# A residue subtraction moved from VectorE to GpSimd for weight pieces of the second block

## The chip, the cores and the metric

The kernel runs on one core of one Trainium2 chip. The metric is the device time of one execution in microseconds (us); less is better. The engines named below are PE (TensorE matmul), PEld (its weight load), DVE (VectorE), ACT (ScalarE), POOL (GpSimd) and SP (SyncE, which only issues transfers here).

## The reference, cut to what matters

Two transformer-like blocks run one after the other on 256 positions of 1024 features, all in float32. The change lies in the mixer of the second block:

```
proj = h @ w_in                     # 1024 x 8224
glu_a, glu_b, q, k, v, z, a_in, b_in, gate_a, gate_b = split_cols(proj, IN_SIZES)
c = glu_a * sigmoid(glu_b)
c = depthwise_conv(c, conv_dw_w) + conv_dw_b          # 31 taps, 1024 channels
c = silu(layer_norm(c)); y_conv = c @ w_conv_out
qkv = silu(depthwise_conv(concat[q, k, v], qkv_conv_w))   # 5 taps
q, k, v -> l2_norm -> gated_delta_rule, forwards and backwards, 8 heads
o = rms_norm(o_fwd + o_bwd) * silu(z); y_delta = o @ w_delta_out
x = x + (sigmoid(gate_a) * y_conv + sigmoid(gate_b) * y_delta) @ w_o
```

## The kernel before, in words

**Weights.** Every weight matrix comes in pieces of 128 x 2048 floats (1 MB): 256 output columns, with the 1024 input features as 8 groups of 128. `Weights.raw` (L177) issues the transfer of a piece on SP (L187) into a `raw` buffer. `Weights.new` (L200) splits the piece into two parts that are multiplied apart: ACT casts `raw` to `hi` (L211), and `lo = raw - hi` is formed on DVE (L212). With `parts=2`, as in the second block, each of these is done in two instructions of 128 x 1024. PE then multiplies both (`mmA`, tiles `mmA<-xs,hi` and `mmA<-xs,lo`): 48 matmuls per piece. In the second block there are two buffers each for `raw`, `hi` and `lo`. A raw buffer can take its next piece once the last reader of the piece before it, which is the second `lo` instruction, has ended. Pieces listed in `NATIVE` are multiplied straight from `raw`.

**Order.** `SEQ` (L33) lists the steps of the second block. A letter is a kind of step and a digit a pair of heads or channels: `g` gates a pair of conv channels (pieces b and a, `glu`), `k` the keys, `p` the queries and values (pieces q and v), `i` the inverse for two heads, `d` the delta rule for two heads, `v` the 31-tap convolution of one tile of 128 channels (`conv31`, taps at L1341), `z`, `x`, `y` gates, `u` the norm of the output, `o` its projection, `l` the norm of the convolution. The entries `rv0`, `rb2`, `rb3`, `rz2` fetch and split a piece ahead of its use: the loop calls `W.split("in2", 2)` itself there and keeps the result in the dictionary `ahead`, from which the inner `split(key)` (L1048) takes it later. The part of the list that matters is `... p1 i0 rb2 g2 i1 d0 v0 p2 v1 i2 d1 rb3 g3 p3 i3 d2 ...`.

The order of instructions on an engine is not that of the code. When the program is built, a planner takes instructions by their place in the code and by costs and due times of its own, so that, for example, the taps of the convolution (L1341) stand between instructions of other steps. Once built, each engine works through its list in order.

**What else is near.** In `inverse(i)` POOL has one `affine_select` for each head (L1185), which sets a diagonal in `U`; ACT copies of it (L1188) and the first matmul of the inverse wait for it. These eight selects are all that POOL does between 631 us and the end of the block. The steps of the inverse go from PE to ACT and DVE and back (`Z` at L1200, `X` at L1208). The `qkv` convolution has its taps at L1078. `ln_y` (L1129 to L1133) is a logarithm over 128 x 32 values. At the end of the block `conv_norm` takes the mean of the convolution with the matmuls `mu<-cv,onesm`, which need all taps.

Of the kernel before, what the change touches and what calls it, by code (L numbers as in the profile page):

```python
# [10 lines left out]
F32 = mybir.dt.float32  # L11
# [4 lines left out]
OP = mybir.AluOpType  # L16
# [17 lines left out]
z0 u0 u1 u2 v2 u3 v5 y0 y1 v3 y2 y3 o v7 l x0 x1 x2 x3""".split()  # L34

NATIVE = ("b0", "a0", "q0", "q1", "z1", "q2", "z0", "k0")
XF, XE, XO, XL = 1, 1, 1, 1
XR = 1
P_NAT, P_UP, P_DN, P_OUT, P_ODD = 2, 1, 2, 2, 2
# [12 lines left out]
def weight_spec():  # L52

    w8 = lambda n, cols: [(n, 0, 8, c, 256) for c in cols]
    halves = lambda n, k0: [(n, k0, 4, 0, 512), (n, k0, 4, 512, 512)]
    s = [("even_in", 0, 8, 1792, 68)] + w8("even_in", (1536, 1860, 2116, 2372, 2628, 2884, 3140))
    s += w8("even_in", (0, 256, 512, 768, 1024, 1280))
    s += halves("even_out", 4) + halves("even_out", 0)
    s += up_down("up0", "down0")
    s += w8("odd_in", (1544,)) + [("odd_in", 0, 8, 1536, 8)] + w8("odd_in", (1800, 2056)) + w8("odd_in", range(0, 1536, 256))  # L60
    s += halves("odd_out", 4) + halves("odd_out", 0)
    s += up_down("up1", "down1")
    first = {"g": "ba", "k": "k", "p": "qv", "z": "z", "x": "x", "y": "y"}
    col = {"a": 0, "b": 1024, "q": 2048, "k": 3072, "v": 4096, "z": 5120, "x": 6176, "y": 7200}
    piece = lambda key: w8("in2", [col[key[0]] + 256 * int(key[1])])
    for q in SEQ:
        if q[0] == "r":
            s += piece(q[1:])
        for c in first.get(q[0], ""):
            if "r" + c + q[1] not in SEQ:  # L70
                s += piece(c + q[1])
        if q == "e":
            s += [("in2", 0, 8, 6144, 32)]
        if q == "o":
            s += w8("delta_out", range(0, 1024, 256))
    s += w8("conv_out", range(0, 1024, 256))
    s += w8("o", range(0, 1024, 256))
    u = up_down("up2", "down2")
    s += u[:2] + [("pl_proj", 0, 2, 0, 1024)] + u[2:]
    s += w8("pl_gate", range(0, 1024, 256))  # L80
    return s
# [72 lines left out]
class Weights:  # L154
# [39 lines left out]

        self.ready.append(self.new(name, parts))

    def split(self, name, parts=1, moving=False):
        return self.ready.pop(0) if self.ready else self.new(name, parts, moving)

    def new(self, name, parts, moving=False):  # L200
        r = self.raw(name)
        nk, w = r.shape[1], r.shape[2]
        hp, lp, kw = self.rings()
        hi = hp.tile([128, WBUF], FR, tag="hi", name=f"hi{self.i}", **kw)
        lo = lp.tile([128, WBUF], FR, tag="lo", name=f"lo{self.i}", **kw)
        o = SWAP if moving else 0
        hi, lo = (t[:, o:o + nk * w].rearrange("p (k c) -> p k c", k=nk) for t in (hi, lo))
        n = -(-nk // parts)
        for a in range(0, nk, n):
            b = min(nk, a + n)  # L210
            self.nc.scalar.copy(hi[:, a:b], r[:, a:b])  # L211
            self.nc.vector.tensor_tensor(lo[:, a:b], r[:, a:b], hi[:, a:b].bitcast(F32), OP.subtract)  # L212
        return hi, lo


# [1 line left out]
def emit(ctx, tc, A):  # L217
    nc = tc.nc
# [9 lines left out]
    W = Weights(nc, A["wts"], weight_spec(), pool("raw", 2), pool("hi", 2), pool("lo", 2))  # L228
# [162 lines left out]
    def rstd_cols(*parts, eps=EPS):  # L391
        m, r = small(2, "rm"), small(2, "rs", 3)
        V.tensor_scalar(m, mean_cols(*parts), eps, None, OP.add)
        rsqrt(r, m, 2)
        return r
# [304 lines left out]
    with ExitStack() as st:  # L700
# [31 lines left out]
        r = rstd_cols(acc)  # L732
# [109 lines left out]
    with ExitStack() as st:  # L842
# [9 lines left out]
        r = rstd_cols(acc)  # L852
# [85 lines left out]
    with ExitStack() as st:  # L938
# [27 lines left out]
        scaled, ahead, turn = [], {}, []  # L966
# [79 lines left out]
            return e  # L1046

        def split(key):  # L1048
            return ahead.pop(key) if key in ahead else W.split("in2", 2)

        def proj(key):

            native = key in NATIVE
            w = W.raw("in2") if native else split(key)
            ps = bank("mm", "mmA")
            for m in range(2):
                if native:
                    mmN(ps[:, T * m:T * m + T], w, hg, m)
                else:
                    mmA(ps[:, T * m:T * m + T], w, xs1, m)  # L1060
            return ps
# [431 lines left out]
    with ExitStack() as st:  # L1493
# [40 lines left out]
        r = rstd_cols(acc)  # L1534
# [87 lines left out]
```

## Time and profile before

| | |
|---|---|
| median of 3 runs | 1235.45 us (1234.9 to 1237.3) |
| the profiled execution's own time | 1236.36 us |
| its span in the trace | 1234.6 us |
| mean granted TensorE clock | 0.991 of full speed |
| DMA over the span | 195.43 MB, mean 158 GB/s |

The span is the stretch from the first to the last instruction of the profiled execution; the execution's own time has 1.8 us around it. Times in the rows are us from the start of the span. A row of the timeline gives the start, the duration, the engine, the line, the operation, the tiles (out<-in), the shape and how many instructions are merged in it; in brackets stands idle time before it and what ended that.

### The profile page before, as it was taken

The numbers are of one execution on the slowest core, as the hardware profiler recorded it, in microseconds if no ns is written. First come the engines' busy times: TensorE is split into PE (matmuls) and PEld (weight loads), VectorE is DVE, ScalarE is ACT, GpSimd is POOL, SyncE is SP. The second block draws the span as 40 slices with busy tenths as digits, with TensorE's granted clock in tenths as the row PEclk, the third lists the DMA queues.
The fourth block names the chain that finished last, engine by engine and source line by source line (L and its number), as shares of the span: only waits on it lengthen the run. The fifth ranks groups of instructions, "written<-read, shape, count | busy, mean of one in ns | idle before, by whom it ended". The sixth has DMA issues, their size and how long they took to land.

```text
span 1234.6 us, 25022 instructions
## 1 busy us (share of the span) xinstructions
PE 1203.5 (97%) x10426; PEld 1149.7 (93%) x10426; DVE 967.8 (78%) x1926; ACT 714.4 (58%) x1185; POOL 12.5 (1%) x21
## 2 busy tenths in 40 slices
PE   8999999999999999999999999999999999999997
PEld 8978899999989899999989998989899999999996
DVE  5986798885597689787559898889998688666556
ACT  4565666664465566665426498898545565444444
POOL 0000000000000000000010000000000000000000
PEclk7999999999999999999999999999999999999999
DMA  5544355545343255555425323212244456555542
GB/s 223 210 150 163 111 205 205 191 173 201 129 169 137 103 205 175 200 187 189 170 81 196 113 105 136 70 36 71 102 137 171 171 201 218 190 204 191 189 167 86
DMA packets 29345, 195.43 MB, mean 158 GB/s; under 512 B 3504, under 2 KB 4016, under 8 KB 9136
## 3 DMA queue, kind: packets, MB, share of 16 engines
q1 hardware_dynamic: 29232, 193.83, 44.3%
q8 instruction: 82, 1.34, 0.4%
q14 instruction: 31, 0.25, 0.1%
HBM read 192.77 MB, written 1.05 MB: 157 GB/s over the span
## 4 chain that ended last, share of the span: by engine, by line
PE 67%; issue 11%; DVE 8%; ACT 5%; POOL 1%; DMA 0%; ACTq 0%; POOLq 0%; DVEq 0%
PE mmU L286 26%; PE mmD L286 15%; PE mmA L286 11%; PE mmB L286 3%; DVE lo L212 3%; PE mmO L286 3%; ACT hi L211 2%; PE mmF L286 2%; PE sr L286 1%; PE do L286 1%; PE at_y L286 1%; PE at_t L289 1%; ACT xbd L1217 1%; PE at_s L286 1%; DVE cv L495 0%
## 5 line engine op out<-in xcount | busy, mean ns | idle before, releaser
L211 ACT CAST hi<-raw 128x1024 fp32r<-128x1024 f32 (+2 forms) x281 | 337.0, 1222 | 299.0 <-PE mmU L286 119.5
L212 DVE TENSOR_TENSOR lo<-raw,hi 128x1024 fp32r<-128x1024 f32 (+2 forms) x281 | 400.5, 1438 | 113.3 <-ACT hi L211 112.6
L286 PE MATMUL mmU<-xs,hi 128*128 128x256 f32 x1996 | 356.2, 278 | 1.9 <-ACT hi L211 1.0
L286 PEld LDWEIGHTS mmU<-xs,hi 128*128 128x128 f32 x1996 | 306.4, 188 | 2.4 <-ACT hi L211 1.1
L286 PE MATMUL mmU<-xs,lo 128*128 128x256 f32 x1056 | 292.9, 278 | 1.4 <-DVE lo L212 1.4
L286 PE MATMUL mmA<-xs,hi 128*128 128x256 f32 x1152 | 220.0, 287 | 0.3 <-ACT hi L211 0.3
L286 PEld LDWEIGHTS mmU<-xs,lo 128*128 128x128 f32 x1056 | 198.2, 188 | 1.9 <-DVE lo L212 1.8
L286 PEld LDWEIGHTS mmA<-xs,hi 128*128 128x128 f32 x1152 | 179.1, 189 | 2.4 <-issue 0.7
L286 PE MATMUL mmD<-hid,hi 128*128 128x256 f32 x1008 | 177.2, 277 | 0.0
L286 PE MATMUL mmA<-xs,lo 128*128 128x256 f32 x576 | 163.1, 283 | 1.3 <-DVE lo L212 1.3
L286 PEld LDWEIGHTS mmD<-hid,hi 128*128 128x128 f32 x1008 | 153.6, 188 | 0.0
L286 PE MATMUL mmD<-hid,lo 128*128 128x256 f32 x528 | 146.1, 277 | 0.0
L286 PEld LDWEIGHTS mmA<-xs,lo 128*128 128x128 f32 x576 | 108.5, 188 | 3.4 <-DVE lo L212 1.9
L1341 DVE SCALAR_TENSOR_TENSOR cv<-cpad,par,cv 128x256 f32<-128x256 f32 x240 | 107.9, 480 | 0.5
L286 PEld LDWEIGHTS mmD<-hid,lo 128*128 128x128 f32 x528 | 99.1, 188 | 0.0
L286 PE MATMUL mmB<-hi,xs 128*128 128x256 f32 x416 | 75.9, 282 | 0.0
L286 PEld LDWEIGHTS mmB<-hi,xs 128*128 128x128 f32 x416 | 64.4, 190 | 0.7 <-issue 0.3
L286 PE MATMUL mmA<-hg,raw 128*128 128x256 f32 x256 | 63.9, 386 | 0.1
L495 DVE SCALAR_TENSOR_TENSOR cv<-mmU,par,cv 128x255 f32<-128x255 f32 (+1 forms) x144 | 61.4, 476 | 1.6 <-ACT cv L493 1.3
L286 PE MATMUL mmB<-lo,xs 128*128 128x256 f32 x208 | 58.6, 282 | 0.0
L286 PEld LDWEIGHTS mmA<-hg,raw 128*128 128x128 f32 x256 | 45.7, 190 | 5.3 <-issue 0.3
L286 PE MATMUL mmO<-xs,hi 128*128 128x256 f32 x256 | 48.0, 286 | 0.5 <-ACT xs L326 0.5
(452 smaller groups left out, 1783.5 us busy)
## 6 DMA issues: line engine op xcount, KB each, us to landing
raw<-in_wts_dram SPq DMA_DIRECT2D x157, 1024.0 KB, 4.8
raw<-in_wts_dram SPq DMA_DIRECT2D x24, 896.0 KB, 4.5
at_l<-in_relb_dram SPq DMA_DIRECT2D x4, 384.0 KB, 9.2
h<-in_xT_dram SPq DMA_DIRECT2D x4, 256.0 KB, 4.0
out_dram<-xg SPq DMA_DIRECT2D x2, 512.0 KB, 2.9
cst<-in_cst_dram SPq DMA_DIRECT2D x1, 640.0 KB, 8.5
buf<-in_g_plp_dram SPq DMA_DIRECT2D x1, 512.0 KB, 5.5
gfin<-in_g_fin_dram SPq DMA_DIRECT2D x1, 512.0 KB, 5.2
```

The source lines that it names most:

```text
L211: self.nc.scalar.copy(hi[:, a:b], r[:, a:b])
L212: self.nc.vector.tensor_tensor(lo[:, a:b], r[:, a:b], hi[:, a:b].bitcast(F32), OP.subtract)
L286: PE.matmul(out, lhsT=lhsT, rhs=rhs, start=start, stop=stop, skip_group_check=True)
L289: PE.transpose(out, in_, ident)
L495: V.scalar_tensor_tensor(y[:, d:], x[:, :T - d], cw[:, 3 * ch + 2 - d:3 * ch + 3 - d], y[:, d:], OP.mult, OP.add)
L1217: S.copy(XT[half[q], :, half[q]], py[half[q]].rearrange("p (n c) -> p n c", n=8))
L1341: V.scalar_tensor_tensor(cv[:, k], cpad[:, k, t:t + T], cw[:, t:t + 1], cv[:, k], OP.mult, OP.add)
```

## The change

A tuple `POOLED` names six pieces of the second block's input projection. `new` and `split` get an argument `eng`, the engine of the `lo` subtraction, which is DVE where it is not given. The inner `split(key)` passes GpSimd for keys in `POOLED`.

```
+POOLED = ("b2", "a2", "v2", "b3", "a3", "v3")
...
-    def split(self, name, parts=1, moving=False):
-        return self.ready.pop(0) if self.ready else self.new(name, parts, moving)
-
-    def new(self, name, parts, moving=False):
+    def split(self, name, parts=1, moving=False, eng=None):
+        return self.ready.pop(0) if self.ready else self.new(name, parts, moving, eng)
+
+    def new(self, name, parts, moving=False, eng=None):
...
-            self.nc.vector.tensor_tensor(lo[:, a:b], r[:, a:b], hi[:, a:b].bitcast(F32), OP.subtract)
+            (eng or self.nc.vector).tensor_tensor(lo[:, a:b], r[:, a:b], hi[:, a:b].bitcast(F32), OP.subtract)
...
         def split(key):
-            return ahead.pop(key) if key in ahead else W.split("in2", 2)
+            return ahead.pop(key) if key in ahead else W.split("in2", 2, False, nc.gpsimd if key in POOLED else None)
```

## Rows read from the trace of the kernel before

**Rows 1.** Windows of the second block: length, then busy us by engine.

```profile
710.00:800.00 90.00, 86.89 (x970) 78.56 (x968) 80.42 (x172) 79.75 (x162) 4.29 (x5) 1.00 0.30 106
800.00:910.00 110.00, 108.66 (x1120) 98.28 (x1119) 100.31 (x253) 78.75 (x150) 2.12 (x3) 1.00 0.20 72
938.00:965.00 27.00, 25.54 (x198) 24.33 (x197) 21.79 (x42) 18.24 (x29) 0.00 (x0) 1.00 0.38 125
```

**Rows 2.** DVE's timeline: lo instructions: b2 (second), a2, v2 (second), a3 (first), v3.

```profile
717.00 1.23 DVE L212 TENSOR_TENSOR lo<-raw,hi 128x1024 fp32r<-128x1024 f32 x1
...
718.99 2.36 DVE L212 TENSOR_TENSOR lo<-raw,hi 128x1024 fp32r<-128x1024 f32 x2
...
738.11 1.22 DVE L212 TENSOR_TENSOR lo<-raw,hi 128x1024 fp32r<-128x1024 f32 x1
...
761.72 1.22 DVE L212 TENSOR_TENSOR lo<-raw,hi 128x1024 fp32r<-128x1024 f32 x1
...
787.77 2.35 DVE L212 TENSOR_TENSOR lo<-raw,hi 128x1024 fp32r<-128x1024 f32 x2
```

**Rows 3.** POOL's timeline: three of the eight selects of the inverse.

```profile
727.96 0.64 POOL L1185 TENSOR_SCALAR_AFFINE_SELECT U<-U 128x512 f32<-128x512 f32 x1 [3.99 <-DVE U L1181]
...
761.87 1.56 POOL L1185 TENSOR_SCALAR_AFFINE_SELECT U<-U 128x512 f32<-128x512 f32 x1 [1.51 <-DVE U L1181]
...
838.04 0.75 POOL L1185 TENSOR_SCALAR_AFFINE_SELECT U<-U 128x512 f32<-128x512 f32 x1 [35.34 <-DVE U L1181]
```

**Rows 4.** DVE's timeline: one operation with and without a select beside it.

```profile
838.20 0.61 DVE L354 TENSOR_TENSOR nw_t<-nw_t,nw_m 128x4 f32<-128x4 f32 x1
...
845.46 0.15 DVE L354 TENSOR_TENSOR nw_t<-nw_t,nw_m 128x4 f32<-128x4 f32 x1
```

**Rows 5.** ACT's timeline: hi casts of a2, v2 (both), a3 (first), v3.

```profile
713.63 2.00 ACT L211 CAST hi<-raw 128x1024 fp32r<-128x1024 f32 x2 [0.18 <-DMA raw<-in_wts_dram]
...
726.84 1.05 ACT L211 CAST hi<-raw 128x1024 fp32r<-128x1024 f32 x1
...
736.78 1.05 ACT L211 CAST hi<-raw 128x1024 fp32r<-128x1024 f32 x1
...
752.84 1.05 ACT L211 CAST hi<-raw 128x1024 fp32r<-128x1024 f32 x1
...
786.40 2.00 ACT L211 CAST hi<-raw 128x1024 fp32r<-128x1024 f32 x2
```

**Rows 6.** DVE's timeline: what runs just after those casts.

```profile
715.03 0.19 DVE L1131 TENSOR_TENSOR ln_y<-ln_y,ln_b 128x32 f32<-128x32 f32 x1
...
727.80 1.01 DVE L1251 TENSOR_TENSOR E<-qk,E 128x384 f32<-128x384 f32 x2
728.73 0.48 DVE L1341 SCALAR_TENSOR_TENSOR cv<-cpad,par,cv 128x256 f32<-128x256 f32 x1
...
739.84 3.64 DVE L1341 SCALAR_TENSOR_TENSOR cv<-cpad,par,cv 128x256 f32<-128x256 f32 x9
...
753.66 1.22 DVE L212 TENSOR_TENSOR lo<-raw,hi 128x1024 fp32r<-128x1024 f32 x1
...
755.18 0.48 DVE L1341 SCALAR_TENSOR_TENSOR cv<-cpad,par,cv 128x256 f32<-128x256 f32 x1
...
790.05 3.25 DVE L1341 SCALAR_TENSOR_TENSOR cv<-cpad,par,cv 128x256 f32<-128x256 f32 x8
794.37 0.16 DVE L1303 COPY oss<-oss 128x4 f32<-128x4 f32 x1 [1.07 <-PE oss L286]
```

**Rows 7.** PE's timeline: b2's lo matmul, the mean's matmuls.

```profile
718.28 0.39 PE L286 MATMUL mmA<-xs,lo 128*128 128x256 f32 x1
...
937.58 3.61 PE L286 MATMUL mu<-cv,onesm 128*128 128x256 f32 x16
```

**Rows 8.** DVE's timeline: the last tap of the convolution.

```profile
937.61 0.48 DVE L1341 SCALAR_TENSOR_TENSOR cv<-cpad,par,cv 128x256 f32<-128x256 f32 x1
```

**Rows 9.** Waits of SP's queue, 710 to 800 us: total us, times, longest.

```profile
SPq L187 <- DVE lo L212: 98.0, 8, 25.6
```

## The prediction

> **What bounds the kernel now.** I read the windows first, then DVE's, POOL's and ACT's timelines around the weight pieces that the change names, then PE's at the places where it needs them, and last the waits of SP's queue. In the windows of the second block no engine stands out: from 710 to 800 us PE is busy 86.89 of 90 us, DVE 80.42 and ACT 79.75 [rows 1]. The inverse and the delta rule hand results from PE to ACT and DVE and back, projections fill PE between them, and convolution taps fill DVE. So PE is close to its limit and DVE is the engine behind it; the PE idle time that could be won back is 3.11 us there and 1.46 us from 938 to 965 us [rows 1]. At the end of the block the two run level: the mean of the convolution starts on PE at 937.58 us and the last tap on DVE at 937.61 us, ending at 938.09 [rows 7, 8]. POOL has 4.29 us of work in 90 [rows 1].
>
> **What really moves.** `POOLED` has six keys, but `b2` and `b3` are fetched by the entries `rb2` and `rb3`. There the loop calls `W.split("in2", 2)` without an engine, and the inner `split(key)` then only takes the finished piece from `ahead`. So these two stay on DVE, and a2, v2, a3 and v3 move: four pieces, eight instructions of 128 x 1024. No transfer is added, and no arithmetic. The transfer that waits for a `lo` to release its raw buffer now waits for POOL instead. SP already waits 98.0 us for `lo` in that stretch, eight times [rows 9]. Of the casts that I use below only one waited for its transfer, 0.18 us [rows 5]; the others wait for buffers and for ACT's own turn, so I charge nothing for a transfer that starts a little later. If that cover were gone, each of the four pieces could delay a cast by what POOL needs more than DVE, some 1.3 us.
>
> **What DVE saves.** The pair of a2 takes 2.36 us and so does that of v3 (2.35); a single one takes 1.22 [rows 2]. Next instructions start a little before the last ends, so I count 1.14 for each. Seven of them give 7.95 us. The eighth, v2's second at 738.11 [rows 2], stands before an idle moment of DVE, which waits for PE there, so its going saves nothing.
>
> **What POOL needs for one.** The trace has no two-input operation on POOL. The nearest row is the select, 0.64 us for 512 elements of one input [rows 3]. If a second input costs nothing, 1024 elements take 1.28 us; if both are read one after the other, 2.56 us. A subtraction reads two tensors, so I take 2.56 and keep 1.28 for the range. The Trainium skill, GPSIMD Engine Reference, section "Elementwise — side-by-side cycle accounting", gives 4497 ns for a two-input operation of 2048 elements, so by an estimate 2.25 us here; by that the sum below would be some 2 us less.
>
> **What POOL does to DVE meanwhile.** This is the term that decides. A select that starts at 761.87, just after a `lo` on DVE at 761.72, takes 1.56 us and not 0.64: it is done about half a us after that `lo` ends at 762.94 [rows 2, 3]. It goes the other way too: a product of 128 x 4 on DVE takes 0.61 us at 838.20, beside the select at 838.04 to 838.79, and 0.15 at 845.46 without one [rows 3, 4]. It is done when the select is. Yet the select at 727.96 runs its 0.64 us beside `E<-qk,E` on DVE, which has one operand in PSUM [rows 3, 6]. So a DVE instruction with two operands in SBUF and a POOL instruction exclude each other, and I let DVE's queue stand at the first such instruction until POOL is done. The Trainium skill, SBUF — State Buffer, section "Who interferes with whom", says that whichever issues first has the shared port for its whole instruction; these rows show it for 0.6 us, and no row for as long as a weight piece.
>
> I go through the eight with the casts as starting times, 1.05 us for one [rows 5], and DVE's list of before [rows 6]:
> - a2: the first cast is done at 714.67, POOL runs to 717.23 and then to 719.79. DVE comes to `ln_y` at 715.03, stands until 717.23 (2.2), gets in a few, and stands again for about 2.0: 4.2 us.
> - v2, first: cast done at 727.89, POOL to 730.45. The tap at 728.73 stands 1.7 us.
> - v2, second: cast done at 737.83, POOL to 740.39. The taps at 739.84 stand 0.55 us.
> - a3, first: cast done at 753.89, but b3's `lo` holds POOL until about 754.8; POOL to 757.4. The tap at 755.18 stands 2.2 us, with b3's second `lo` behind it.
> - a3, second: DVE then has only work with a PSUM operand, so nothing.
> - v3: the first cast is done at 787.4. POOL to 790.0 and 792.6. The eight taps, which move up from 790.05 to 787.77, stand 2.2 and 2.6 us: 4.8 in all.
>
> Together 13.5 us of standing against 7.95 saved: DVE is 5.5 us later. The idle 1.07 us before the copy at 794.37 [rows 6] takes up that much, which leaves 4.4. At the end PE comes to the last of the eight `mu` products some 2.7 us after the last tap is done (937.58 and 3.61 us for them all, the last eighth from about 940.7, against 938.09) [rows 7, 8], so a delay that falls on taps alone costs 4.4 - 2.7 = 1.7 us. A delay that falls on the steps of the inverse, or on PE itself, costs all 4.4. The first part is of the second kind: behind the standing `ln_y` is b2's own second `lo`, which ends at 718.23, and PE takes it at 718.28 [rows 2, 7]; there is no slack, and PE's list stands with it. I take the middle of the two, 3 us.
>
> **Sum.** 1236.36 us of the profiled execution + 3 = 1239.4. The median of the runs is 0.9 below that execution, so 1238.5 us. About 0.2% (2.5 us) is what a measurement of this kernel can tell from no change.
>
> **The rivals.**
> - *No measurable change.* Stalls fall on taps, which can wait, and the planner, which orders each engine's list anew with POOL's cost in view, puts PSUM work beside POOL. For it: three of the five places where DVE stands are taps [rows 6], and after 800 us 9.7 of DVE's 110 us are idle [rows 1]. Against it: b2's `lo` at 718.23. It gives 1236 us, anything within 2.5 of the median.
> - *Faster.* POOL needs about 1.28 us, or its reads let DVE through. With 1.28 the standing shrinks to about 0.9 + 0.7 (a2), 0.4 (v2), 0.9 (a3) and 2.2 (v3), 5.1 us, against 7.95 saved: DVE gains 2.8, and with no standing 7.95. PE can use no more than its idle 3.11 + 1.46 = 4.6 us [rows 1], so between 2.8 and 4.6 us: 1232 us, at the lowest 1231. It decides below about 1.7 us per instruction on POOL, where standing and saving are level. Against it stand the doubled duration of the select and the 0.61 us [rows 3, 4].
> - *Much slower.* DVE stands through all eight: 8 x 2.56 = 20.5, less 7.95 and the 1.07 of idle: 11.5 us, 1247 us. For it: POOL's two go back to back, so DVE may not get between. Against it: work with a PSUM operand goes on.
>
> That the planner orders the lists anew moves each of these by a few us either way, which no row shows; it widens all.
>
> **How the numbers follow.** Slower by 2.5 to 8 us 0.36, by more 0.07; no measurable change 0.31; faster 0.26. So faster 0.26, same 0.31, slower 0.43. The likeliest is slower, 1238.5, with 1238 to 1243 as its own range. To leave out no more than 2 in 10 the range takes in the lowest of faster, 1231, and nearly all of much slower, 1246.
>
> **What would show it.** POOL's `lo` should be eight instructions of 2.3 to 2.8 us, longer beside a DVE `lo`; twelve of them would mean that b2 and b3 move as well. Taps or small two-input operations on DVE should show 1 to 2.5 us in place of 0.48 and 0.15 beside them; if they keep their durations, the exclusion is wrong and the faster rival gains. b2's second `lo` should end after 718.23 and PE's matmul with it. The last tap should end at 939 to 943 us. A last tap before 936 us, or PE idle below 3 us from 710 to 800, would make the prediction wrong.

## The result and the profile after

The changed kernel takes 1246.93 us in the median of 4 runs (1244.61 to 1249.90), the kernel before 1235.33 beside it. The ratio of the times is 1.0081, 95% interval 1.0064 to 1.0098: slower, by 10.0 us as the ratio has it and 11.6 by the two medians. The execution that was profiled took 1246.88 us, its span is 1245.0. All line numbers of the second block are 2 higher than before: the taps are L1343, `lo` is L214, `hi` L213, PE's matmuls L288.

First the windows of the second block of the kernel after, in the columns of [rows 1], and the waits of PE in the first of them (total us, times, longest):

```profile
710.00:800.00 90.00, 77.87 (x880) 70.80 (x880) 82.06 (x155) 69.41 (x138) 22.32 (x12) 0.96 0.27 96
800.00:910.00 110.00, 108.64 (x1116) 97.53 (x1115) 99.72 (x243) 77.08 (x157) 2.55 (x4) 1.00 0.20 68
```

```profile
PE ivy L288 <- DVE Z L1202: 3.5, 2, 1.9
PE mmA L288 <- DVE cpad L1080: 3.4, 1, 3.4
PE sr L288 <- ACT ws L1269: 2.1, 2, 1.8
PE ivx L288 <- DVE Z L1202: 1.4, 1, 1.4
PE sv L288 <- DVE r L1276: 1.1, 1, 1.1
```

From 710 to 800 us PE is idle for 12.13 us (90 less 77.87), against 3.11 [rows 1]; from 800 to 910 nothing has changed. Four of these five longest waits name DVE, and no wait of PE in this window names a `lo` of POOL. Yet DVE's busy time rose, from 80.42 to 82.06, although it runs fewer instructions there, 155 against 172. POOL's and DVE's timelines show why:

```profile
712.32 4.68 POOL L214 TENSOR_TENSOR lo<-raw,hi 128x1024 fp32r<-128x1024 f32 x2 [83.68 <-DVE ln_y L1132]
...
730.18 2.52 POOL L214 TENSOR_TENSOR lo<-raw,hi 128x1024 fp32r<-128x1024 f32 x1
738.57 2.35 POOL L214 TENSOR_TENSOR lo<-raw,hi 128x1024 fp32r<-128x1024 f32 x1 [5.86 <-ACT hi L213]
760.93 4.89 POOL L214 TENSOR_TENSOR lo<-raw,hi 128x1024 fp32r<-128x1024 f32 x2 [20.01 <-ACT hi L213]
...
788.28 2.46 POOL L214 TENSOR_TENSOR lo<-raw,hi 128x1024 fp32r<-128x1024 f32 x1 [16.46 <-PE ivy L288]
791.47 2.35 POOL L214 TENSOR_TENSOR lo<-raw,hi 128x1024 fp32r<-128x1024 f32 x1 [0.72 <-ACT hi L213]
```

```profile
712.63 2.12 DVE L1133 TENSOR_TENSOR ln_y<-ln_y,ln_b 128x32 f32<-128x32 f32 x1
714.67 0.47 DVE L1080 SCALAR_TENSOR_TENSOR cpad<-mmA,par,cpad 128x255 f32<-128x255 f32 x1
715.06 1.98 DVE L1135 TENSOR_TENSOR ln_y<-ln_y,ln_n 128x32 f32<-128x32 f32 x1
...
717.56 0.86 DVE L1080 SCALAR_TENSOR_TENSOR cpad<-mmA,par,cpad 128x254 f32<-128x254 f32 x2
718.35 1.21 DVE L214 TENSOR_TENSOR lo<-raw,hi 128x1024 fp32r<-128x1024 f32 x1
...
729.24 3.75 DVE L1343 SCALAR_TENSOR_TENSOR cv<-cpad,par,cv 128x256 f32<-128x256 f32 x3
...
739.00 3.38 DVE L1343 SCALAR_TENSOR_TENSOR cv<-cpad,par,cv 128x256 f32<-128x256 f32 x4
742.31 0.67 DVE L1202 TENSOR_TENSOR Z<-ivp,lev 128x512 f16<-128x512 f32 x1
...
762.56 1.02 DVE L1343 SCALAR_TENSOR_TENSOR cv<-cpad,par,cv 128x256 f32<-128x256 f32 x1
...
763.90 2.20 DVE L1343 SCALAR_TENSOR_TENSOR cv<-cpad,par,cv 128x256 f32<-128x256 f32 x1
...
786.83 4.19 DVE L1343 SCALAR_TENSOR_TENSOR cv<-cpad,par,cv 128x256 f32<-128x256 f32 x5
...
791.55 4.53 DVE L1343 SCALAR_TENSOR_TENSOR cv<-cpad,par,cv 128x256 f32<-128x256 f32 x6
```

Eight `lo` run on POOL, so four pieces moved and not six. At each of them DVE stands. `ln_y` with two operands in SBUF takes 2.12 and 1.98 us in place of 0.19 [rows 6]; it ends when POOL's instruction ends (POOL's first is done at 714.70, the first `ln_y` at 712.63 + 2.12 = 714.75; POOL's second at 717.00, the second `ln_y` at 717.04). The taps with one operand in PSUM (`cpad<-mmA`) keep their 0.47 us between the two. A tap on `cv` takes 0.48 us alone, and eight take 3.25 and nine 3.64 [rows 6], so each further one 0.39; three in 3.75 us are 2.49 too long, four in 3.38 1.73, five in 4.19 2.15 and six in 4.53 2.10. With 1.93 and 1.79 at `ln_y`, and 0.54 and 1.72 at the taps beside a3, the rows above show 14.5 us of standing. (Of the 2.49 some 0.4 lie beside a select.) POOL's own selects are not held up by its new work: each of the four before 800 us starts after POOL has been idle for 1.29 us or more, until DVE gives `U`.

What this does to PE is seen in its timeline:

```profile
713.46 1.28 PE L288 MATMUL qk<-qT,kT 128*128 128x128 f32 x10
718.18 0.48 PE L288 MATMUL mmA<-xs,hi 128*128 128x256 f32 x2 [3.45 <-DVE cpad L1080]
...
739.13 0.44 PE L288 MATMUL ivy<-id,Z 64*64 64x64 f16 x16 [1.55 <-DVE Z L1202]
...
743.04 0.21 PE L288 MATMUL ivy<-xbd,Z 64*64 64x64 f16 x1 [1.91 <-DVE Z L1202]
...
746.74 1.22 PE L288 MATMUL mmA<-hg,raw 128*128 128x256 f32 x2
...
946.77 3.61 PE L288 MATMUL mu<-cv,onesm 128*128 128x256 f32 x16
```

At 714.74 PE's projection needs a PSUM bank that DVE reads (`cpad<-mmA`); those reads stand in DVE's queue behind the two long `ln_y`, and PE waits 3.45 us. At 741.13 the inverse needs `Z`, which DVE gives at 742.98, after four taps that should have taken 1.65 us and took 3.38; PE waits 1.91 us. And the granted clock of TensorE falls after it:

```profile
740.00:743.70 3.70, 1.79 (x10) 1.15 (x10) 3.70 (x7) 2.15 (x6) 0.92 (x1) 1.00 0.48 124
743.70:750.60 6.90, 6.90 (x53) 6.29 (x52) 3.93 (x11) 2.89 (x7) 0.00 (x0) 0.51 0.45 158
750.60:755.00 4.40, 4.40 (x77) 3.81 (x77) 3.07 (x8) 3.93 (x8) 0.00 (x0) 1.00 0.30 128
```

The granted clock (the column after POOL's busy time) falls from 1.00 (2.4 GHz) to 0.51 (the level of 1.2 GHz) for 6.9 us behind the two stops of 1.55 and 1.91 us; from 740 to 743.7 us, with the second of them, PE was busy for 1.79 of 3.7 us. Two matmuls `mmA<-hg,raw` take 1.22 us there and 0.60 at 736.99. Before, the clock was at 1.00 in all windows of [rows 1].

**The balance.** The casts of a2 start on ACT at 711.19 us, 2.44 earlier than before [rows 5]; the mean's matmuls `mu` start on PE at 946.77, 9.19 later than before [rows 7]. Between the two 11.6 us are lost: 12.13 - 3.11 = 9.0 of idle time, and the rest, 2.6, fits the half clock (at most half of 6.9 us, 3.5). The earlier start comes from the first 40 us of the program, where the granted clock was 0.85 from 5 to 40 us, against 0.80 in the execution before; the change is not what I can put it down to.

### The profile page after: what moved, and what is told of

The parts are those of the page before. It is cut to its first block, busy times and chain, and to the rows that moved or that the text cites. A ratio compares the mean times of both kernels' runs of the same rounds, so it can differ in the third digit from the quotient of the medians.

```text
span 1245.0 us, 25018 instructions
## 1 busy us (share of the span) xinstructions
PE 1204.6 (97%) x10426; PEld 1151.4 (92%) x10426; DVE 972.6 (78%) x1918; ACT 709.8 (57%) x1181; POOL 31.0 (2%) x29
## 4 chain that ended last, share of the span: by engine, by line
PE 73%; DVE 10%; ACT 5%; issue 2%; POOL 1%; DMA 0%; ACTq 0%; DVEq 0%; POOLq 0%
PE mmU L288 26%; PE mmA L288 15%; PE mmD L288 15%; PE mmB L288 3%; PE mmO L288 3%; DVE lo L214 3%; DVE cv L1343 2%; PE mmF L288 2%; ACT hi L213 1%; PE sr L288 1%; PE do L288 1%; PE at_y L288 1%; DVE cpad L1080 1%; PE at_t L291 1%; PE ss L288 1%
## 5 line engine op out<-in xcount | busy, mean ns | idle before, releaser
L213 ACT CAST hi<-raw 128x1024 fp32r<-128x1024 f32 (+2 forms) x281 | 337.2, 1222 | 300.5 <-PE mmU L288 126.9
L214 DVE TENSOR_TENSOR lo<-raw,hi 128x1024 fp32r<-128x1024 f32 (+2 forms) x273 | 391.0, 1445 | 114.3 <-ACT hi L213 113.7
L288 PE MATMUL mmU<-xs,hi 128*128 128x256 f32 x1996 | 355.9, 278 | 1.9 <-ACT hi L213 1.0
L288 PEld LDWEIGHTS mmU<-xs,hi 128*128 128x128 f32 x1996 | 306.2, 188 | 2.4 <-ACT hi L213 1.1
L288 PE MATMUL mmU<-xs,lo 128*128 128x256 f32 x1056 | 292.8, 278 | 2.0 <-DVE lo L214 2.0
L288 PE MATMUL mmA<-xs,hi 128*128 128x256 f32 x1152 | 218.4, 287 | 3.9 <-DVE cpad L1080 3.4
L288 PEld LDWEIGHTS mmU<-xs,lo 128*128 128x128 f32 x1056 | 198.3, 188 | 2.5 <-DVE lo L214 2.4
L288 PEld LDWEIGHTS mmA<-xs,hi 128*128 128x128 f32 x1152 | 179.3, 189 | 6.2 <-issue 4.3
L288 PE MATMUL mmD<-hid,hi 128*128 128x256 f32 x1008 | 177.2, 277 | 0.0
L288 PE MATMUL mmA<-xs,lo 128*128 128x256 f32 x576 | 165.4, 287 | 1.3 <-DVE lo L214 1.3
L288 PEld LDWEIGHTS mmD<-hid,hi 128*128 128x128 f32 x1008 | 153.7, 188 | 0.0
L288 PE MATMUL mmD<-hid,lo 128*128 128x256 f32 x528 | 146.1, 277 | 0.0
L1343 DVE SCALAR_TENSOR_TENSOR cv<-cpad,par,cv 128x256 f32<-128x256 f32 x240 | 116.7, 523 | 0.3
L288 PEld LDWEIGHTS mmA<-xs,lo 128*128 128x128 f32 x576 | 109.1, 189 | 3.1 <-DVE lo L214 1.7
L288 PEld LDWEIGHTS mmD<-hid,lo 128*128 128x128 f32 x528 | 99.1, 188 | 0.0
L288 PE MATMUL mmB<-hi,xs 128*128 128x256 f32 x416 | 75.4, 281 | 0.0
L288 PEld LDWEIGHTS mmB<-hi,xs 128*128 128x128 f32 x416 | 64.0, 188 | 0.7 <-issue 0.3
L288 PE MATMUL mmA<-hg,raw 128*128 128x256 f32 x256 | 64.0, 388 | 0.1
L288 PE MATMUL mmB<-lo,xs 128*128 128x256 f32 x208 | 58.2, 280 | 0.0
L288 PEld LDWEIGHTS mmA<-hg,raw 128*128 128x128 f32 x256 | 46.0, 191 | 5.3 <-issue 0.3
L288 PE MATMUL mmO<-xs,hi 128*128 128x256 f32 x256 | 48.1, 286 | 0.5 <-ACT xs L328 0.5
```

The source lines that it names most:

```text
L214: (eng or self.nc.vector).tensor_tensor(lo[:, a:b], r[:, a:b], hi[:, a:b].bitcast(F32), OP.subtract)
L288: PE.matmul(out, lhsT=lhsT, rhs=rhs, start=start, stop=stop, skip_group_check=True)
L1343: V.scalar_tensor_tensor(cv[:, k], cpad[:, k, t:t + T], cw[:, t:t + 1], cv[:, k], OP.mult, OP.add)
```

## The experiments

Three theories stood against each other. The exclusion: POOL's reading stops DVE's two-operand instructions, and these stop PE. The late `lo`: POOL needs more than twice as long for a piece, so PE, or the transfer that waits for the raw buffer, gets it late. The lists: the planner knows POOL's cost and orders every engine's list anew, and the new order is worse. Each ratio below is to the kernel before on the same chip, in three rounds; "standing" is the sum over all DVE instructions from 700 to 830 us of what each takes above the median of its form in the kernel before (0.4 us there, 14.8 in the kernel after), added up from the trace; the longest stop is the largest such excess of a single instruction (2.14 us in the kernel after).

**The reading without the moving.** DVE forms all `lo`, as before; POOL reads as much beside it, with a result that nobody uses. The edit, here and below against the changed kernel:

```
-            (eng or self.nc.vector).tensor_tensor(lo[:, a:b], r[:, a:b], hi[:, a:b].bitcast(F32), OP.subtract)
+            self.nc.vector.tensor_tensor(lo[:, a:b], r[:, a:b], hi[:, a:b].bitcast(F32), OP.subtract)
+            if eng:
+                eng.tensor_tensor(self.scr, hi[:, a:b].bitcast(F32), self.con, OP.subtract)
...
```

Two lines are left out here; they set `scr`, the place of the result in the tail of the `cpad` buffer, and `con`, 1024 constants in `cst`.

> DVE forms every lo as before. For a2, v2, a3 and v3 POOL also does two subtractions of 128 x 1024 with two SBUF operands (hi and constants) whose result nobody reads. Theory 1, exclusion (DVE stands at instructions with two SBUF operands while POOL reads): DVE saves nothing and stands some 13 us, so slower than before by 10 to 20 us, taps and small products of 1 to 2.5 us beside the subtractions. Theory 2, lateness (the slower lo on POOL holds PE and the transfers back): no change, within 2 us. Theory 3 (the planner's new lists alone): slower by about the same 11 us as the change, but with no long taps.

Measured: ratio 1.0115 (1.0091 to 1.0140), 1250.84 us against 1237.62. That is 13.2 us by the medians and 14.2 by the ratio, lost though DVE still forms every `lo` and POOL's result has no reader. So a late `lo`, for which no change was expected, is not the cause here. Nor is the order of the instructions: by operation, tiles and shape the lists of this kernel are those of the kernel before, but for one of DVE's 1926 instructions, two of ACT's 1185 and a handful of PE's. Two effects of the reading itself are in the figure beside DVE's standing: the `hi` buffer is held longer, and two selects queue on POOL behind a read that ends at 768.79 us, for which PE waits 2.44 us (`ubd`, which ACT copies from them); the changed kernel has no such wait. DVE stands 14.0 us, the longest stop 2.17. POOL's and DVE's timelines of this kernel around a2, and around v3 where the two engines' weight pieces meet:

```profile
714.12 4.87 POOL L216 TENSOR_TENSOR cpad<-hi,cst 128x1024 bf16<-128x1024 f32 x2 [84.23 <-ACT hi L213]
...
796.70 5.69 POOL L216 TENSOR_TENSOR cpad<-hi,cst 128x1024 bf16<-128x1024 f32 x2 [25.75 <-ACT hi L213]
```

```profile
714.62 1.99 DVE L1139 TENSOR_TENSOR ln_y<-ln_y,ln_n 128x32 f32<-128x32 f32 x1
716.53 0.47 DVE L1084 SCALAR_TENSOR_TENSOR cpad<-mmA,par,cpad 128x255 f32<-128x255 f32 x1
716.93 2.10 DVE L1140 TENSOR_TENSOR gneg<-gneg,ln_y 128x32 f32<-128x32 f32 x1
...
796.88 6.60 DVE L214 TENSOR_TENSOR lo<-raw,hi 128x1024 fp32r<-128x1024 f32 x2
```

The stops at `ln_y` and `gneg` are those of the changed kernel, one instruction later. At 796.88 DVE's own pair of `lo` takes 6.60 us where it took 2.35 [rows 2].

**The saving without the reading.** POOL fills the four pieces' `lo` with zeros, so that DVE's eight instructions are gone and POOL only writes:

```
-            (eng or self.nc.vector).tensor_tensor(...)
+            if eng:
+                eng.memset(lo[:, a:b].bitcast(F32), 0.0)
+            else:
+                self.nc.vector.tensor_tensor(...)
```

> POOL only writes zeros into the lo tiles of a2, v2, a3 and v3 (the residue of these four pieces is left out), so it reads nothing. DVE is freed of the same eight subtractions. Theory 1, exclusion: DVE does not stand, the 11 us are gone, between 5 us faster and 2 us slower than before; taps stay at 0.48 us. Theory 2, lateness: also no loss, since the zeros are there early. Theory 3, planner's new lists: still slower by 5 us or more.

Measured: ratio 0.9982 (0.9971 to 0.9993), 1234.96 us against 1237.62. So all that DVE gains by the eight instructions is worth 2.2 us by the ratio (0.18% of 1237.6; 0.9 to 3.6 by its interval), 2.7 by the medians. That may be too much, since the zeros wait neither for the transfer nor for the cast. DVE stands 0.8 us in it. Its windows, and POOL's and DVE's timelines at the first pair:

```profile
710.00:800.00 90.00, 87.55 (x987) 80.47 (x986) 80.86 (x190) 78.26 (x157) 10.42 (x13) 1.00 0.31 108
```

```profile
713.29 1.94 POOL L215 MEMSET lo<- 128x1024 f32 x2 [82.71 <-PE mmA L291]
```

```profile
713.01 1.24 DVE L217 TENSOR_TENSOR lo<-raw,hi 128x1024 fp32r<-128x1024 f32 x1
714.14 0.19 DVE L1135 TENSOR_SCALAR ln_y<-ln_y 128x32 f32<-128x32 f32 x1
714.23 0.49 DVE L1083 SCALAR_TENSOR_TENSOR cpad<-mmA,par,cpad 128x254 f32<-128x254 f32 x1
714.62 0.20 DVE L1134 TENSOR_TENSOR ln_y<-ln_y,ln_x 128x32 f32<-128x32 f32 x1
```

While POOL writes from 713.29 to 715.23, DVE's `lo` and `ln_y` with two operands in SBUF keep their times. PE is idle 2.45 us. The Trainium skill, SBUF — State Buffer, section "Who interferes with whom", says that a DVE instruction with two SBUF inputs contends with a GpSimd instruction that reads SBUF and not with one that only writes it. These two kernels agree: 14.0 us of standing and a ratio of 1.0115 by the first, 0.8 us and 0.9982 by the second. The planner's new lists alone are not the loss either: compared as above, 96% of DVE's list stands here in the order of the changed kernel, 87% in that of the kernel before, and nothing is lost.

**All six pieces.** The prefetched b2 and b3 are given to POOL as well:

```
-                ahead[q[1:]] = W.split("in2", 2)
+                ahead[q[1:]] = W.split("in2", 2, False, nc.gpsimd if q[1:] in POOLED else None)
```

> b2 and b3 move to POOL too, so twelve subtractions there. Theory 1: half as much standing again on DVE, slower than before by 14 to 20 us, unless b2's own second lo, which stands behind ln_y on DVE in the change, was most of the loss; then below 11 us. Theory 2: b2, which PE takes at once, comes later by 2 to 5 us, slower by 14 to 20 us.

Measured: ratio 1.0151 (1.0130 to 1.0172), 1255.87 us against 1237.62. POOL has four more such instructions from 700 us on, DVE stands 23.3 us, PE is busy 76.00 of the 90 us. The two more pieces cost some 8.7 us (18.7 by the ratio, less 10.0), nearly as much as the first four. Both theories had 14 to 20 us here, so this run doesn't tell them apart.

**One piece at a time.** `POOLED` is cut to one key, `("a2",)`, `("v2",)`, `("a3",)` or `("v3",)`, and then to two, `("a2", "v2")`.

> Only a2's two subtractions on POOL. By the prediction's terms a2 makes DVE stand 4.2 us and saves 2.3, with b2's second lo behind it: 2 to 4 us slower than before. Theory 1 by the changed kernel's trace: the two ln_y products stand 2.1 and 2.0 us, 2 to 5 us slower. Theory 2 (lateness of a2's lo): PE takes it 2 us after it is there in the changed kernel, so no change.

> Only v2's two subtractions on POOL. By the prediction's terms 0.6 + 0.55 us. By the changed kernel's trace the delay between the first select of the inverses 0 and 1 grows by 8 us; if v2's standing taps ahead of Z and the drop of the TensorE clock that follows make that, 5 to 9 us slower than before with a stretch at half clock; if the drop needs a2's stop as well, 1 to 4 us.

> Only a3's two subtractions on POOL. By the prediction's terms about 0 (1.05 less 1.13). Theory 1: 0 to 3 us slower. Theory 2: no change, the lo is early.

> Only v3's two subtractions on POOL. By the prediction's terms 4.8 of standing less 2.3 and 1.07 of idle, 1.4 us slower. Theory 1 by the changed kernel's trace (Z and r behind standing taps, the delay grows by 2.3 us): 1 to 4 us slower. Theory 2: no change, PE takes v3 12 us later.

> a2 and v2 on POOL together. Alone a2 cost 2.0 us and v2 nothing to -1.4 us. If costs of pieces simply add, 0 to 3 us slower than before. If v2's standing taps hurt only behind a2's delay (as the changed kernel's trace looks: PE stops 1.55 and 1.91 us for Z there, and a half-clock stretch follows), 5 to 9 us slower.

| pieces on POOL | ratio (95%) | worked out, us | DVE stands, us (longest) | PE busy of 710 to 800 us | half clock, us |
|---|---|---|---|---|---|
| none (before) | | | 0.4 (0.37) | 86.89 | 0 |
| a2 | 1.0016 (1.0002 to 1.0029) | +2.0 | 4.5 (2.05) | 84.48 | 3.4 |
| v2 | 0.9989 (0.9975 to 1.0002) | -1.4 | 4.4 (2.09) | 85.99 | 0 |
| a3 | 1.0020 (1.0005 to 1.0035) | +2.5 | 1.7 (1.69) | 86.20 | 3.4 |
| v3 | 1.0027 (1.0014 to 1.0040) | +3.3 | 4.4 (2.09) | 84.27 | 6.8 |
| a2, v2 | 1.0057 (1.0041 to 1.0074) | +7.0 | 8.6 (2.10) | 81.60 | 6.8 |
| four (after) | 1.0081 (1.0064 to 1.0098) | +10.0 | 14.8 (2.14) | 77.87 | 6.8 |

The column worked out is the ratio's difference from 1 times 1237.8 us (1236.8 for the pair, 1235.3 for the last row); the last column is the time from 100 to 1225 us of the profiled execution in which the granted clock was at 0.50. DVE's standing adds up by pieces: 4.5 + 4.4 + 1.7 + 4.4 = 15.0, against 14.8. For time that doesn't hold from piece to piece: a2 and v2 alone give 2.0 - 1.4 = 0.6, together 7.0. The lowest of the first four ratios, v2's, is a tie with the kernel before, where I had expected 1 to 9 us. So 4.4 us of standing, nearly all on taps, cost nothing measurable, net of the two instructions saved. PE's own waits show what differs; these lines are PE's waits from 710 to 800 us with v2 alone, then with a2 and v2:

```profile
PE ivy L288 <- DVE Z L1202: 1.7, 2, 1.1
```

```profile
PE mmA L288 <- DVE cpad L1080: 3.6, 1, 3.6
PE ivy L288 <- DVE Z L1202: 3.4, 2, 1.9
```

With v2 alone the inverse's PE matmuls wait 1.7 us for `Z`, with the two together 3.4, and the granted clock falls to half from 749.8 to 753.2 us (before that from 722.4 to 725.9), which it does nowhere between 100 and 1225 us with v2 alone. Why the same piece stops `Z` for longer when a2 is there too is not settled: each kernel has its own order of instructions, so this part may belong to the lists. The clock goes with the loss: v2 alone, the kernel that only writes and the kernel before have no half clock in that stretch, and each kernel with a loss clear of zero has some (10.2 us in the first experiment, 13.7 with all six pieces). It costs at most half its length: up to 1.7 us with a2 or a3 alone, 3.4 with v3.

**Reading one input.** As the first experiment, but POOL only copies `hi`:

```
...
+            if eng:
+                eng.tensor_copy(self.scr, hi[:, a:b].bitcast(F32))
...
```

> As the run in which POOL only reads, but POOL copies hi alone, one SBUF operand, so each of the eight takes about half as long (1.0 to 1.3 us). DVE still forms every lo. Exclusion: DVE stands for as long as POOL reads, so about half the 14 us: 4 to 9 us slower than before. If two operands on POOL are needed for the exclusion, or if the extra instructions' place in the lists made the loss: no change, or 10 us and more.

Measured: ratio 1.0014 (1.0001 to 1.0028), about 1.7 us. POOL takes 1.04 us for 128 x 1024; DVE stands 4.7 us, the longest stop 0.83. I had expected 4 to 9 us. The order on DVE, ACT and PE is, compared as above, the same as in the first experiment, instruction by instruction; only POOL's reads are shorter. The lines are POOL's first two reads, and `ln_y` and `gneg` on DVE, at the place where the first experiment had 1.99 and 2.10 us:

```profile
715.80 2.16 POOL L216 CAST cpad<-hi 128x1024 bf16<-128x1024 f32 x2 [84.82 <-ACT hi L213]
```

```profile
716.26 0.64 DVE L1139 TENSOR_TENSOR ln_y<-ln_y,ln_n 128x32 f32<-128x32 f32 x1
716.82 0.47 DVE L1084 SCALAR_TENSOR_TENSOR cpad<-mmA,par,cpad 128x255 f32<-128x255 f32 x1
717.22 0.78 DVE L1140 TENSOR_TENSOR gneg<-gneg,ln_y 128x32 f32<-128x32 f32 x1
```

So the stop is as long as what is left of POOL's instruction, and a third of the standing costs an eighth of the time (by the two intervals, between nothing and a third).

**Shorter instructions.** All four pieces on POOL, as in the changed kernel, but in quarters:

```
-        n = -(-nk // parts)
+        n = -(-nk // (4 if eng else parts))
```

> The change with its POOL subtractions cut into 128 x 512, and ACT's casts with them: sixteen POOL instructions of about 1.2 us. If only the sum of POOL's reading time counts, as slow as the change, 8 to 12 us above before. If the length of one stop counts (a Z or a bank release behind one long stop), DVE gets in between and the loss falls to 3 to 7 us.

Measured: ratio 1.0027 (1.0012 to 1.0042), about 3.3 us against 10.0. The reading is the same, in sixteen instructions of 128 x 512; ACT's casts of these pieces are in quarters too, and the lists are new again. POOL's first four of them, and what DVE does meanwhile:

```profile
711.93 5.00 POOL L214 TENSOR_TENSOR lo<-raw,hi 128x512 fp32r<-128x512 f32 x4 [83.44 <-ACT hi L213]
```

```profile
712.00 1.30 DVE L1132 TENSOR_SCALAR ln_y<-ln_y 128x32 f32<-128x32 f32 x1
713.21 0.47 DVE L1080 SCALAR_TENSOR_TENSOR cpad<-mmA,par,cpad 128x255 f32<-128x255 f32 x1
713.61 0.93 DVE L1133 TENSOR_TENSOR ln_y<-ln_y,ln_b 128x32 f32<-128x32 f32 x1
```

DVE still stands 11.7 us, 3.1 less than with halves, but no single stop is above 1.11 us, and PE is busy 83.57 of 90 us in place of 77.87. Most of the loss is gone though four fifths of the standing are left, so the sum alone doesn't set it. At a2 the sum still counts: four short stops follow each other there, PE waits 3.0 us for the bank in place of 3.45, and the clock is at half from 716.6 to 723.5 us, worth up to 3.4 us. What shrank are the waits for `Z`, from 3.5 and 1.4 us in all to 1.1 and 0.6. That the length of the stops did it is the likely reading; the finer casts and the other order are not separated from it.

No kernel tried computes the whole and is measurably faster than the kernel before.

## Why the prediction came out as it did

The direction was right, slower, and so was the mechanism of the stops, where and for how long DVE stands; what the stops cost was not: 3 us were forecast over the profiled execution, and about 10 were lost. The prediction gave more than 8 us a chance of 0.07, and the measured time lies at the very edge of its range, 1246 us (1246.9 by the median, 1245.3 by the ratio), which went so far only for the sake of a rival. The sign came out of a difference whose terms were both mis-sized, so some luck is in it. Step by step:

- *What moves.* Right: eight instructions, a2, v2, a3 and v3. b2 and b3 stay; giving them to POOL as well cost some 8.7 us more.
- *Transfers charged at nothing.* Nothing speaks against it: SP now waits for POOL's `lo`, and the only cast at which the profile shows a wait for a transfer around the moved pieces waited 0.23 us (0.18 before [rows 5]).
- *POOL's 2.56 us for one.* Nearly right: 2.34 to 2.55 us in the profile. With one input, in a copy to bf16, the same elements took 1.04 us, so the second input is not free. The estimate of 2.25 from the Trainium skill's page GPSIMD Engine Reference, section "Elementwise — side-by-side cycle accounting", was as near, from below. The faster rival's 1.28 us falls.
- *The exclusion, 13.5 us of standing.* Right as a sum (14.5 in the rows above) and nearly by piece: 3.7 for a2 (4.2 forecast), 2.5 and 1.7 for v2 (1.7 and 0.55), 2.3 for a3 (2.2, all of it put at the first instruction, where 0.54 fell, and 1.72 at the second), 4.3 for v3 (4.8). The Trainium skill's rule of whole instructions, in SBUF — State Buffer, section "Who interferes with whom", now has rows for stops of 2.1 us.
- *"Together 13.5 us of standing against 7.95 saved: DVE is 5.5 us later."* This step failed. The two are not of one kind. The saving alone, with writes only, was worth 2.2 us; PE, idle for 3.11 us of that stretch [rows 1], had little more to win. The reading alone cost 13.2 us by the medians and 14.2 by the ratio, 2.4 of them by selects that queue behind it on POOL. The one less the other is 13.2 - 2.7 = 10.5 us by the medians and 14.2 - 2.2 = 12.0 by the ratios; measured were 11.6 and 10.0. That they come so near is in part chance, since each kernel's stops fall in other places. (Seven times 1.14 is 7.98, not 7.95; nothing hangs on it.)
- *What a delay costs, 1.7 to 4.4 and "the middle of the two, 3 us".* The term that was mis-sized follows from that step; it came to about 10. I took the tap's lateness at the end of the block as the measure, with 2.7 us of slack. But the last tap was not late: it ends at 930.65 us, against 938.09 [rows 8], while the mean's matmuls that take them come at 946.77. I had written that a last tap before 936 us would make the prediction wrong; what it made wrong is this argument. A tap can wait, but not what stands behind it in DVE's queue, `Z` and the read that frees a PSUM bank. The taps were the place where DVE stood, not the place where it was felt.
- *"Three of the five places where DVE stands are taps."* By the prediction's own list four are, and of the eight stops measured six. Taps were the usual case, as this rival had it, but in the changed kernel `Z` stood behind some of them.
- *"Behind the standing `ln_y` is b2's own second `lo`" and "there is no slack".* The place was right and the item wrong: PE stopped there for 3.45 us, but for the PSUM bank that `cpad<-mmA` frees; b2's second `lo` starts at 718.35, after PE has gone on at 718.18.
- *Not in the sum at all:* the granted clock, which fell to half after two such stops for 6.9 us and cost up to 3.5 us here.
- *Much slower, through all eight.* Its 11.5 us came near the time by luck: DVE gets work with a PSUM operand in between, as forecast, and stands 14 us and not 20.5.

What stays open is how much of the changed kernel's loss its new order adds or saves. The order isn't needed for a loss: the first experiment keeps that of the kernel before and loses more. But that pieces do not add up says that the order has a part in where each stop is felt, and no run here changes the order alone.

## What to carry to other kernels

Before an elementwise operation goes to GpSimd, count two things apart: what the freed engine can really use (here 2.2 of 8 us), and each DVE instruction with two operands in SBUF that will stand while GpSimd reads, with what is queued behind it; a us of the one is not a us of the other. A stop costs by what stands behind it in the queue: v2's 4.4 us alone cost nothing measurable, net of the saving, and a2's stop held up a PSUM bank for 3.45 us. If the work has to be moved, short instructions lose less (quarters in place of halves: 3.3 us and not 10.0), though still more than not moving it. DVE's taps with an operand in PSUM went on at 0.47 us beside POOL; to place the work beside those was not tried.

## What the runs showed of the hardware

- A DVE instruction with a single input tensor can stand too: the `ln_y` TENSOR_SCALAR of 128 x 32 at 712.00 in the kernel with quarters took 1.30 us beside POOL's 128x512, and 0.18 elsewhere; with all six pieces on POOL two of them took 2.37 and 2.31. I had counted two-operand instructions alone. The Trainium skill, SBUF — State Buffer, section "Who interferes with whom", lists tensor_scalar among the operations that can take the shared ports too; no run here shows whether that is the reason.
- Where both engines have two-operand instructions in a row they hinder each other: POOL's two reads at 796.70 in the first experiment took 5.69 us in place of 4.87, and DVE's pair of `lo` beside them 6.60 in place of 2.35 [rows 2].
- POOL's writes are free for DVE: MEMSET of 128x1024 took 0.95 to 1.04 us, with DVE at its usual times.
- TensorE's clock doesn't follow the length of a stop alone. In the kernel after it was at 1.00 from 718 to 725 us, right behind the stop of 3.45 us, and fell behind two of 1.55 and 1.91. With a2 alone on POOL the stop in the same place (3.54 us, to 718.08) went with half clock from 717.6 to 721.0. What tells the two apart is not settled. The windows of the kernel after and of the one with a2 alone:

```profile
718.00:725.00 7.00, 6.82 (x60) 6.76 (x61) 7.00 (x17) 6.24 (x14) 0.41 (x1) 1.00 0.78 300
```

```profile
717.60:721.00 3.40, 2.92 (x14) 2.96 (x15) 3.40 (x7) 3.35 (x6) 0.00 (x0) 0.50 0.71 251
```
